# A hybrid decoder trunk on one core: output projection by seven products, gate rank inside the gate's block, norms without transposes

## The chip, the core and the metric

The program runs on one core of one Trainium2 chip. The metric is device time in microseconds (us) of one execution. The core has a matrix engine (PE), a vector engine (DVE), a scalar engine (ACT), a general engine (POOL) and a synchronisation engine (SP); each works through its own list of instructions in order, and one that waits on a semaphore holds up everything behind it on that engine. Copies between DRAM and the on-chip memory are issued by SP or POOL and carried by 16 DMA engines that all queues share.

## The reference

One layer on 1024 tokens of width 2048, all in float32. Three groups of heads read the same normed input through one wide projection `w_in`; their outputs are normed per head, gated, and go through one output projection. Then come a cross attention over 256 memory tokens and a last norm.

```python
h = rmsnorm(x, norm_mix)
(sb_q, sb_k, sb_v, sb_g, gla_q, gla_k, gla_v, gla_r, gla_g,
 sgu_u, sgu_v, sgu_g) = split(h @ w_in)          # widths 4 x 1024, 256, 256, 512, 16, 512, 3 x 512
o_sb  = stick_breaking_attention(sb_q, sb_k, sb_v)               # 8 heads of 128
log_alpha = log_sigmoid(gla_r @ w_gla_gate_up + b_gla_gate) / 16
o_gla = gla_chunked(gla_q, gla_k, gla_v, log_alpha)
o_sgu = chunked_sgu(gelu(sgu_u), gelu(sgu_v), sgu_norm, w_sgu, b_sgu)
mix  = rmsnorm per head (concat[o_sb, o_gla, o_sgu])
gate = silu(concat[sb_g, gla_g, sgu_g])
x = x + (mix * gate) @ w_out                                     # 1024 x 2048 by 2048 x 2048
x = x + memory_cross_attention(rmsnorm(x, norm_xattn), rmsnorm(mem, norm_mem), w_xq, w_xkv, w_xo)
return rmsnorm(x, final_norm)
```

## The kernel before

**Arithmetic.** Every float32 operand of a large product is kept as a rounded part and a remainder (`split_to`: a copy on ACT, then a subtraction on DVE), and a product is three matmuls (`mm3`), each with a stationary block of 128x128 and 512 moving columns. Weights come from DRAM in pieces of 128x512 (256 KB) on SP's queue into three buffers `wr`, and are split into three pairs of buffers `wh`, `wl`.

**Stages.** `natural(acts, w3, c0, width, evac)` computes 512 columns of `acts @ w3` for all 1024 tokens in eight PSUM banks: 16 steps, one weight piece each, of 24 matmuls with the activations stationary. The program runs through (1) the loads of the transposed input, its norm, and the first values of two head groups in 64 half-steps of 12 matmuls, one weight piece each; (2) five natural blocks over `w_in`: the second half of the attention's values, then `su`, `sv`, `sg` and the gate `gg`, each stored to DRAM from SBUF; (3) keys and values of the memory; (4) column blocks for the other groups, woven with their chunked work, where `gla_rank` computes the 16 rank columns with 64 matmuls whose output has 32 rows; (5) eight attention heads; (6) the output projection in four chunks of 512 columns, whose result plus `x` is stored to `x2_scr` (`evac_chunk`); (7) the second norm, which loads `x2` rows back, scales them on DVE and turns them with 128 PE transposes (`norm2_turn`), half of it inside the last chunk and half inside the first query block; (8) two query blocks, the cross attention, and 32 output steps of 12 matmuls with a norm of each group of 128 rows (`out_step`, `out_norm_step`).

**What sets the order.** `weave` writes PE's order by hand: a list of steps, and tasks that are due at a step number (`later`). PE keeps exactly that order. The order on the other engines, SP's queue of DMA issues among them, is made by a scheduler when the program is built: an instruction stands where that scheduler expects it to be ready, which is not always where the code has it. At run time each engine keeps the order that it was given.

Of the kernel before, what the change touches and what calls it, by code (L numbers as in the profile page):

```python
# [8 lines left out]
F32 = mybir.dt.float32  # L9
# [8 lines left out]
P = 128  # L18
# [23 lines left out]
def trunk(ctx, tc, x, mem, w_in, w_gla_gate_up, sgu_norm, w_sgu, w_out, w_xq, w_xkv, w_xo, final_norm,  # L42
          xT, memT, cols_in, out, dbg=None):
# [3 lines left out]
    x2d, mem2d, out2d = x[0], mem[0], out[0]  # L47
# [9 lines left out]
    actp = ctx.enter_context(tc.tile_pool(name="actp", bufs=16))  # L57
# [12 lines left out]
    def slot(dt=F32R, name="slot"):  # L70
        return actp.tile([P, 4, 512], dt, tag="act", name=name)
# [31 lines left out]
    layout = (("out", 16), ("xat", 16), ("mem", 16), ("bg", 2), ("bs", 4))  # L103
# [156 lines left out]
    def natural(acts, w3, c0, width, evac, order=range(KT)):  # L260
        for load, steps in row_block(acts, w3, c0, width, evac, [(k, range(ST)) for k in order]):
            load()
            steps[0]()

    class Stage:


        def __init__(self, name, bufs=1):
            self.args, self.pool = dict(name=name, bufs=bufs), None
# [11 lines left out]

    v_scr = [scratch(f"v_scr{s}", [P, 8, 2, P]) for s in range(ST)]
    nat_scr = {nm: [scratch(f"{nm}{s}", [P, 512]) for s in range(ST)] for nm in ("su", "sv", "sg", "gv", "gg")}
    kt_scr = [scratch(f"kt{m}", [P, 4, P]) for m in range(2)]
# [4 lines left out]
    x2_scr = [scratch(f"x2{s}", [P, D]) for s in range(ST)]  # L289
# [47 lines left out]
    with tc.tile_pool(name="st0", bufs=2) as st0:  # L337
# [87 lines left out]
        natural(hT, w_in3, SB_V + 512, 512, evac_v(st0, 512, 4, tag="vt"))  # L425
        last = [None]
        for nm, c0, func in (("su", SG_U, AF.Gelu_apprx_tanh), ("sv", SG_V, AF.Gelu_apprx_tanh),
                             ("sg", SG_G, AF.Silu), ("gg", GL_G, AF.Silu)):
            natural(hT, w_in3, c0, 512, evac_nat(nm, func))
# [120 lines left out]
    def gla_open():  # L550
# [15 lines left out]
        wup = gp.tile([32, 256], F32, name="wup")  # L566
        for i in range(2):
            sp.dma_start(wup[16 * i:16 * i + 16, :], w_gla_gate_up[0])
        wr = gp.tile([P, KT, 16], F32, tag="e", name="wr16", bufs=3)
        sp.dma_start(wr, w_in3[:, :, GL_R:GL_R + 16])  # L570

        wr2 = gp.tile([P, KT, 32], F32R, tag="e", name="wr32", bufs=3)
        split_to(wr2[:, :, 0:16], wr2[:, :, 16:32], wr)
# [5 lines left out]
        rr = gp.tile([32, S], F32, name="rr")  # L579
        gl.update(masks=masks, ind=ind, wup=wup, wr2=wr2, state=state, ql=ql, rr=rr)  # L580

    def gla_rank(h, k0):
        if k0 == 0:
            gl["rb"] = bank("z")
        b = gl["rb"]
        for k in range(k0, k0 + 4):
            for i in range(2):
                mm(b[:32, :], gl["wr2"][:, k, :], hT.at(k, h)[i], k == 0 and i == 0, k == KT - 1 and i == 1)
        if k0 + 4 == KT:
            dve.tensor_copy(gl["rr"][:, h * 512:h * 512 + 512], b[:32, :])  # L590
# [150 lines left out]
    for j in range(8):  # L741
        later(43 + j, gla_rank, j // 4, 4 * (j % 4))
# [182 lines left out]
    ss_x2 = const.tile([P, ST, 4], F32, name="ss_x2")  # L925
    op = Stage("op", 3)
    mT = Operand()
    order = list(range(8, 16)) + list(range(8))

    def mixed(k, h):  # L930

        sl = slice(h * 512, h * 512 + 512)
        if (k // 4, h) not in mT.t:
            mT.t[k // 4, h] = (slot(), slot())
        if k >= 8:
            t = wraw.tile([P, 512], F32, tag="wr", name="mraw")
            sp.dma_start(t, mix_scr[k - 8][:, sl])
        else:
            t = op.tile([P, 512], F32, tag="mraw", name="mraw", bufs=4)
# [36 lines left out]
    for n in (1, 2):  # L976
        natural(mT, w_out3, n * 512, 512, evac_chunk(n), order=order)
# [218 lines left out]
```

## Time and profile before

| | |
|---|---|
| three timed runs | 2161.27, 2162.8, 2168.68 us; median 2162.8 |
| profiled execution | 2166.49 us, its span in the trace 2164.6 us |
| granted PE clock, mean | 0.995 |
| PE busy | 2108.2 us, 97% of the span, 10000 records |
| weight loads on PE | 1735.2 us, beside the matmuls |
| DVE, ACT, POOL busy | 1077.2, 890.6, 186.3 us |
| moved by DMA | 242.66 MB, mean 112 GB/s |

Busy times of different engines overlap and do not add up to the span. A matmul's record is longer than the distance to the next one, since matmuls are pipelined; the distance between starts is what a matmul costs. Loading a weight block runs beside the matmul before it.

### The profile page before, as it was taken

To read this page: it belongs to the slowest core of one execution; us is meant where nothing else is said; L and a number is where in the kernel's file an instruction comes from. 1 tells how busy PE (TensorE), PEld (TensorE's weight loads), DVE (VectorE), ACT (ScalarE), POOL (GpSimd) and SP (SyncE) were. 2 spreads that over 40 slices of the span, in tenths; PEclk is the share of its full clock that TensorE was granted. 3 is DMA by queue.
4 is the path that set the end of the run, shared out by engine and by line. 5 is a ranking of instruction groups with operands and counts; after the bars stand their busy time and mean duration, and the time that the engine had idled before them with its cause. 6 is when DMAs were issued, how large, how long until landed. Compare 5 with 4: busy or idle time off the path is not lost.

```text
span 2164.6 us, 27461 instructions
## 1 busy us (share of the span) xinstructions
PE 2108.2 (97%) x10000; PEld 1735.2 (80%) x10000; DVE 1077.2 (50%) x1978; ACT 890.6 (41%) x1975; POOL 186.3 (9%) x271
## 2 busy tenths in 40 slices
PE   7999999999999999999999999999999999999997
PEld 6788888888887767878888888888877878888886
DVE  8593121111115737375377677776753121377675
ACT  7463111121225432342366665665654121356553
POOL 6200000000000210101110111111012000000001
PEclk9999999999999999999999999999999999999999
DMA  6486132221237521312221222222267231665632
GB/s 210 137 266 210 49 127 59 78 88 49 88 101 235 171 52 40 107 34 89 78 62 52 56 64 57 59 57 56 80 203 234 63 123 49 199 198 168 223 118 98
DMA packets 183111, 242.66 MB, mean 112 GB/s; under 512 B 17568, under 2 KB 99008, under 8 KB 180800
## 3 DMA queue, kind: packets, MB, share of 16 engines
q1 hardware_dynamic: 173760, 232.52, 34.5%
q0 software_dynamic: 9216, 8.39, 1.7%
q8 instruction: 79, 1.29, 0.3%
q14 instruction: 56, 0.46, 0.1%
HBM read 191.56 MB, written 49.28 MB: 111 GB/s over the span
## 4 chain that ended last, share of the span: by engine, by line
PE 43%; DVE 9%; ACT 5%; issue 5%; DMA 2%; POOL 1%; SPq 0%; DVEq 0%; POOLq 0%; ACTq 0%
PE pj L166 31%; PE z L166 6%; PE av L166 4%; DVE a L839 1%; PE tr L171 1%; DVE a L845 1%; ACT t L833 1%; ACT t L834 1%; PE tr L166 1%; DVE t L835 1%; ACT a L846 1%; DMA mraw<-mix 1%; DVE ql L637 1%; ACT t L832 1%; DVE wl L135 1%
## 5 line engine op out<-in xcount | busy, mean ns | idle before, releaser
L135 DVE TENSOR_TENSOR wl<-wr,wh 128x512 fp32r<-128x512 f32 x408 | 297.4, 730 | 715.8 <-ACT wh L134 707.8
L166 PE MATMUL pj<-slot,wh 128*128 128x512 f32 x2048 | 577.1, 398 | 0.5 <-DVE qT L135 0.5
L134 ACT CAST wh<-wr 128x512 fp32r<-128x512 f32 x408 | 252.2, 618 | 747.6 <-PE av L166 518.8
L166 PE MATMUL pj<-wh,slot 128*128 128x512 f32 x1536 | 478.6, 393 | 0.0
L166 PEld LDWEIGHTS pj<-slot,wh 128*128 128x128 f32 x2048 | 370.2, 189 | 71.1 <-issue 2.3
L166 PEld LDWEIGHTS pj<-wh,slot 128*128 128x128 f32 x1536 | 291.8, 190 | 60.6 <-DVE slot L139 0.3
L166 PE MATMUL pj<-slot,wl 128*128 128x512 f32 x1024 | 327.2, 390 | 0.0
L166 PE MATMUL pj<-wl,slot 128*128 128x512 f32 x768 | 304.2, 396 | 17.3 <-DVE wl L135 10.7
L166 PEld LDWEIGHTS pj<-slot,wl 128*128 128x128 f32 x1024 | 192.2, 188 | 42.5
L166 PE MATMUL z<-wh,slot 128*128 128x512 f32 x640 | 197.9, 390 | 0.1
L166 PEld LDWEIGHTS pj<-wl,slot 128*128 128x128 f32 x768 | 145.8, 190 | 51.6 <-DVE wl L135 15.1
L166 PEld LDWEIGHTS z<-wh,slot 128*128 128x128 f32 x640 | 120.2, 188 | 25.8 <-DVE slot L135 0.9
L166 PE MATMUL z<-wl,slot 128*128 128x512 f32 x320 | 125.6, 392 | 4.8 <-DVE xo L956 3.5
L835 DVE SCALAR_TENSOR_TENSOR t<-z,t 128x384 f32<-128x384 f32 (+2 forms) x96 | 53.5, 557 | 94.0 <-ACT t L834 93.9
L166 PE MATMUL tr<-wh,slot 128*128 128x512 f32 x320 | 98.6, 389 | 0.0
L166 PE MATMUL av<-wh,slot 128*128 128x512 f32 x320 | 98.5, 389 | 0.0
L846 ACT ACTIVATE a<-a 128x384 f32<-128x384 f32 (+2 forms) x96 | 50.4, 525 | 114.9 <-DVE a L845 114.8
L166 PE MATMUL pj<-slot,oT 128*128 128x512 f32 x384 | 90.9, 392 | 0.0
L166 PEld LDWEIGHTS pj<-slot,oT 128*128 128x128 f32 x384 | 70.9, 188 | 14.2
L166 PEld LDWEIGHTS z<-wl,slot 128*128 128x128 f32 x320 | 60.1, 188 | 19.7 <-DVE xo L956 4.3
L166 PE MATMUL z<-kT,qT 128*128 128x512 f32 (+3 forms) x288 | 71.2, 355 | 0.0
L166 PEld LDWEIGHTS tr<-wh,slot 128*128 128x128 f32 x320 | 60.1, 188 | 12.4
(252 smaller groups left out, 2647.7 us busy)
## 6 DMA issues: line engine op xcount, KB each, us to landing
wr<-in_w_in_dram SPq DMA_DIRECT2D x256, 256.0 KB, 2.8
wr<-in_w_out_dram SPq DMA_DIRECT2D x88, 256.0 KB, 3.1
xt<-in_xT_dram SPq DMA_DIRECT2D x64, 256.0 KB, 3.9
v_scr<-vt SPq DMA_DIRECT2D x16, 512.0 KB, 3.6
wr<-in_w_xkv_dram SPq DMA_DIRECT2D x32, 256.0 KB, 3.1
v<-v_scr POOLq DMA_DIRECT2D x64, 128.0 KB, 2.8
xr<-in_x_dram SPq DMA_DIRECT2D x32, 256.0 KB, 5.8
x<-xo SPq DMA_DIRECT2D x32, 256.0 KB, 4.0
```

The lines of the kernel that those rows point to most:

```text
L134: act.copy(hi, src)
L135: eng.tensor_tensor(out=lo, in0=src, in1=f32(hi), op=ALU.subtract)
L166: i = pe.matmul(o, l, r, start=start, stop=stop)
L171: i = pe.transpose(o, i_, ident)
L637: dve.tensor_tensor(out=gl["ql"][r_, :, hh, :].rearrange("p c (b i) -> p c b i", i=h), in0=gl["q"][r_, :].rearrange("p (c b i) -> p c b i" ...
L832: act.activation(tw, z, AF.Abs)
L833: act.activation(tw, tw, AF.Exp, scale=-1.0)
L834: act.activation(tw, tw, AF.Ln, bias=1.0)
L835: dve.scalar_tensor_tensor(out=tw, in0=z, scalar=0.0, in1=tw, op0=ALU.max, op1=ALU.add)
L839: dve.tensor_tensor_scan(out=aw[:, ::-1], data0=tw[:, ::-1], data1=tw[:, ::-1], initial=init, op0=ALU.add, op1=ALU.max)
L845: dve.tensor_tensor(out=aw, in0=z, in1=aw, op=ALU.subtract)
L846: act.activation(aw, aw, AF.Exp)
```

## The change

**Output projection.** The product of the 1024x2048 activations with the 2048x2048 weights is cut into 2x2 quarters and done by seven products of quarters instead of eight (`PRODUCTS`), in the order 4, 7, 1, 5, 3, 6, 2. Weights are now the stationary operand and the output comes out transposed. Each product has 16 steps of 12 matmuls of 512 columns. Five of the seven need a sum or difference of two weight quarters. Those are made ahead, in 80 pieces: two loads of 256 KB on SP into `ws` (three buffers for each of the two), an add on POOL (L464), and a store of 256 KB to `sums_scr` issued by POOL (L465). The code asks for one piece at each step of the natural blocks (`beside`). Five products need a sum of two activation quarters, which POOL makes (`as`). Four accumulators per token half and column half lie in SBUF, are preloaded with the transposed input (`sum_open`) and take each product's result by DVE (`collect`, 96 adds); banks of a product's second half first go through a copy on ACT (`ev`).

**Gate rank.** The 16 rank columns lie beside the gate's 512 in `w_in`, so the gate block becomes two blocks of 272 and 256 columns; 8 transposes bring the rank columns into the form that the 64 matmuls gave.

**Norms.** `x2` arrives transposed, so the second norm's gain is applied while it is split (`arrive2`), the sum of squares is made by POOL adds and one matmul with a matrix of ones per half (`scales2`), and the scale itself is applied after the query product. The output steps are transposed too: 64 pairs of products with 256 moving columns, and a last norm by matmuls with ones. The program writes its output transposed.

The instruction lists of the two programs differ by these counts on PE: 958 fewer matmuls of 512 columns with 128 rows of output, 64 fewer with 32 rows, 128 fewer transposes of 128x128, 8 more transposes with 16 rows of output, 384 more matmuls of 272 columns and 1168 more of 256 columns. DMAs issued by SP go from 892 to 1098.

```diff
+    sums_scr = {p: scratch(f"sums{p}", [8, P, 1024]) for p in PRODUCTS if PRODUCTS[p][3]}
...
-        natural(hT, w_in3, SB_V + 512, 512, evac_v(st0, 512, 4, tag="vt"))
+        pending = []
+        sums = Stage("sums", 3)
+        sums.open()
+
+        def sum_pieces():
+            for kk in range(8):
+                for prod in (4, 7, 1, 3, 6):
+                    for j in range(2):
+                        ts = []
+                        for i, (kh, nh) in zip("ab", PRODUCTS[prod][2]):
+                            t = sums.tile([P, 512], F32, tag=f"sum{i}", name="ws")
+                            c0 = nh * 1024 + j * 512
+                            sp.dma_start(t, w_out3[:, kh * 8 + kk, c0:c0 + 512])
+                            ts.append(t)
+                        pending.append((ts, prod, kk, j))
+                        yield
+
+        def sum_store():
+            ts, prod, kk, j = pending.pop(0)
+            pool.tensor_tensor(out=ts[0], in0=ts[0], in1=ts[1], op=PRODUCTS[prod][3])
+            pool.dma_start(sums_scr[prod][kk, :, j * 512:j * 512 + 512], ts[0])
+
+        pieces = sum_pieces()
+
+        def beside():
+            next(pieces, None)
+            if len(pending) > 1 or pending and not pieces.gi_frame:
+                sum_store()
+        natural(hT, w_in3, SB_V + 512, 512, evac_v(st0, 512, 4, tag="vt"), beside=beside)
         for nm, c0, func in (("su", SG_U, AF.Gelu_apprx_tanh), ("sv", SG_V, AF.Gelu_apprx_tanh),
-                             ("sg", SG_G, AF.Silu), ("gg", GL_G, AF.Silu)):
-            natural(hT, w_in3, c0, 512, evac_nat(nm, func))
+                             ("sg", SG_G, AF.Silu)):
+            natural(hT, w_in3, c0, 512, evac_nat(nm, func), beside=beside)
+        def evac_gg(lead):
+            def f(s, b):
+                t = st0.tile([P, 512], F32, tag="nt", name="nt", bufs=4)
+                if lead:
+                    dve.tensor_copy(t[:, 256:272], b[:, :16])
+                    sp.dma_start(rank_scr[:, s, :], t[:, 256:272])
+                last[0] = act.activation(t[:, :256], b[:, lead:], AF.Silu)
+                c = 0 if lead else 256
+                sp.dma_start(nat_scr["gg"][s][:, c:c + 256], t[:, :256])
+            return f
+        natural(hT, w_in3, GL_R, 272, evac_gg(16), beside=beside)
+        natural(hT, w_in3, GL_G + 256, 256, evac_gg(0), beside=beside)
+        while pending:
+            sum_store()
+        sums.close()
...
-    def gla_rank(h, k0):
-        if k0 == 0:
-            gl["rb"] = bank("z")
-        b = gl["rb"]
-        for k in range(k0, k0 + 4):
-            for i in range(2):
-                mm(b[:32, :], gl["wr2"][:, k, :], hT.at(k, h)[i], k == 0 and i == 0, k == KT - 1 and i == 1)
+    def gla_rank(h):
+        tp = bank("z")
+        for i in range(4):
+            flip(tp[:16, i * P:i * P + P], gl["rank"][:, 4 * h + i, :])
+        dve.tensor_copy(gl["rr"][:, h * 512:h * 512 + 512], tp[:16, :])
...
     def mixed(k, h):
 
         sl = slice(h * 512, h * 512 + 512)
-        if (k // 4, h) not in mT.t:
-            mT.t[k // 4, h] = (slot(), slot())
+        t = mix_at(k, h)
         if k >= 8:
             sp.dma_start(t, mix_scr[k - 8][:, sl])
-            t = op.tile([P, 512], F32, tag="mraw", name="mraw", bufs=4)
-            g_ = op.tile([P, 512], F32, tag="graw", name="graw", bufs=4)
+            g_ = op.tile([P, 512], F32, tag="ev", name="graw")
             sp.dma_start(t, on_scr[k][:, sl])
             sp.dma_start(g_, g_scr[k][:, sl])
             last[0] = act.activation(g_, g_, AF.Silu)
             pool.tensor_tensor(out=t, in0=t, in1=g_, op=ALU.mult)
-        split_to(*mT.at(k, h), t)
-
-    def evac_chunk(n):
-        xr = {}
-
...
+    def sum_open(sh, nh):
+        for g in range(2):
+            sp.dma_start(home(SUM[sh, nh][g], "sum", F32), xT3[:, 8 * nh + 4 * g:8 * nh + 4 * g + 4, sh * 512:sh * 512 + 512])
+    FINAL = {(0, 0): 5, (0, 1): 3, (1, 0): 2, (1, 1): 2}
...
+    def prepare_weight(u, prod, kk, j, early):
...
+        def fetch():
+            t = op.tile([P, 512], F32, tag="ra", name="ra") if j and not early else \
+                wraw.tile([P, 512], F32, tag="wr", name="ra")
+            c0 = j * 512
+            if sign:
+                sp.dma_start(t, sums_scr[prod][kk, :, c0:c0 + 512])
+            else:
+                (kh, nh), = quarters
+                sp.dma_start(t, w_out3[:, kh * 8 + kk, nh * 1024 + c0:nh * 1024 + c0 + 512])
+            raws.append(t)
...
+        def split():
+            if j and not early:
+                hl = tuple(op.tile([P, 512], F32R, tag=f"w1{i}", name="w1", bufs=2) for i in "hl")
...
+            wp[u] = hl
+        later(u - (3.2 if early else 6), fetch)
+        later(u - (1.2 if early else 2.8), split)
+
+    def prepare_operand(u, prod, kk):
...
+        def add():
+            st.append(op.tile([P, 512], F32, tag="as", name="as", bufs=2))
+            a, b = (mix_at(kh * 8 + kk, sh) for sh, kh in quarters)
+            pool.tensor_tensor(out=st[0], in0=a, in1=b, op=sign)
...
+        def split():
+            src = st[0] if sign else mix_at(quarters[0][1] * 8 + kk, quarters[0][0])
+            hl = tuple(op.tile([P, 512], F32R, tag=f"a{i}", name="a") for i in "hl")
+            split_to(hl[0], hl[1], src)
+            ap[u] = hl
+        if sign:
+            later(u - 5, add)
+        later(u - 3, split)
...
+    def product_pass(u0, prod, js, tags):
...
+        def step(u, kk, j):
+            w = wp.pop(u)
+            a = a4(kk) if prod == 4 else ap[u - j]
+            for i in range(4):
+                b = 4 * j + i
+                if kk == 0:
+                    banks[b] = bank(tags[b % len(tags)])
+                mm3(banks[b], cut(w, i * P, i * P + P), a, kk == 0, kk == 7)
+                if kk == 7:
+                    collect(prod, b, banks[b], len(js) == 2 and j == 1)
...
+    def collect(prod, b, z, through):
+        if through:
+            t = op.tile([P, 512], F32, tag="ev", name="ev")
+            act.copy(t, z)
+            z = t
+        for (sh, nh), sign in PRODUCTS[prod][4]:
+            d = sum_at(sh, nh, b)
+            dve.tensor_tensor(out=d, in0=d, in1=z, op=sign)
+            if FINAL[sh, nh] == prod:
+                n = 8 * nh + b
+                sp.dma_start(x2_scr[sh][n // 4][:, n % 4], d)
+
+    FOUR, EIGHT = ("pj",) * 4, NAT
+    groups += product_pass(END, 4, (0,), FOUR) + product_pass(END + 8, 4, (1,), ("z", "z", "tr", "av"))
+    for n, prod in enumerate((7, 1, 5, 3, 6)):
+        groups += product_pass(END + 16 + 16 * n, prod, (0, 1), EIGHT)
+    groups += product_pass(W2, 2, (0, 1), EIGHT)
+    for j in range(8):
+        later(END - 12 + j, mixed, 8 + j, 1)
+        later(END - 3 + 0.6 * j if j < 4 else END + j - 3.5, lambda j=j: split_to(*a4(j), mix_at(8 + j, 1)))
+        later(END + 2 + j, mixed, 8 + j, 0)
+        later(END + 18 + j, mixed, j, 0)
+        later(END + 34 + j, mixed, j, 1)
+    later(END + 3, sum_open, 0, 0)
+    later(END + 5, sum_open, 1, 0)
+    later(END + 18, sum_open, 0, 1)
+    later(END + 20, sum_open, 1, 1)
...
+    def arrive2(k, h):
+
+        st = op if h == 0 else xp
+        t = st.tile([P, 512], F32, tag="x2t", name="x2t", bufs=3 + h)
+        sp.dma_start(t, x2_scr[h][k // 4][:, k % 4])
+
+        def f():
+            hi, lo = h2_at(k, h)
+            split_gain(hi, lo, t, col("xat", k))
+            if k == 0:
+                sq_sum[h] = xr.tile([P, 512], F32, tag="acc", name="acc")
+                act.activation(sq_sum[h], t, AF.Square)
+            else:
+                sq = st.tile([P, 512], F32, tag="sq", name="sq", bufs=3)
+                act.activation(sq, t, AF.Square)
+                pool.tensor_tensor(out=sq_sum[h], in0=sq_sum[h], in1=sq, op=ALU.add)
...
+    def scales2(h):
+        st = bank("z")
+        mm(st, ones_f, sq_sum[h], True, True)
+        t = xr.tile([P, 512], F32, tag="t", name="t")
+        R[h] = xr.tile([P, 512], F32, tag=f"R{h}", name="R")
+        inverse_rms(R[h], st, sq_sum[h], R[h], t)
...
-                mm3(banks[h], cut(w[k], h * P, h * P + P), h2T.at(k, half), k == 0, k == KT - 1)
+                mm3(banks[h], cut(w[k], h * P, h * P + P), h2_at(k, half), k == 0, k == KT - 1)
             if k == KT - 1:
                 for h in range(4):
+                    u = xa.tile([P, 512], F32, tag="e", name="qu", bufs=3)
                     t = tuple(xa.tile([P, 512], F32R, tag="qT", name="qT", bufs=8) for _ in range(2))
-                    split_to(t[0], t[1], banks[h])
+                    dve.tensor_tensor(out=u, in0=banks[h], in1=R[half], op=ALU.mult)
+                    split_to(t[0], t[1], u)
...
+    def out_step(p, jj):
         b = bank("pj")
...
+        for i in range(2):
+            j = 2 * jj + i
+            for h in range(4):
+                c = (h % 2) * 256
+                mm3(b[:, i * 256:i * 256 + 256], cut(wxo[h, j // 4], j % 4 * P, j % 4 * P + P),
+                    cut(oT[p, h // 2], c, c + 256), h == 0, h == 3)
+        x3 = fin_at(p, jj // 2)[:, jj % 2 * 2:jj % 2 * 2 + 2]
+        b3 = b.rearrange("p (a s) -> p a s", a=2)
+        dve.tensor_tensor(out=x3, in0=b3, in1=x3, op=ALU.add)
...
+        acc, sq = temp(p % 2), temp(2 + (jj % 2 if jj < 7 else 2 + p % 2))
+        to = acc if jj == 0 else sq
+        act.activation(to.rearrange("p (a s) -> p a s", a=2), x3, AF.Square)
+        if 0 < jj < 7:
+            pool.tensor_tensor(out=acc, in0=acc, in1=sq, op=ALU.add)
+        for i in range(2):
+            act.activation(x3[:, i], x3[:, i], AF.Copy, scale=col("fin", 2 * jj + i))
+
+    def out_norm_step(p):
+        st = bank("z")[:, :256]
+        parts = [t[:, i * 256:i * 256 + 256] for t in (temp(p % 2), temp(4 + p % 2)) for i in range(2)]
+        for n, t in enumerate(parts):
+            mm(st, ones_f, t, n == 0, n == 3)
+        a, c = temp(6), temp(7)
+        v, y, t, r = a[:, :256], a[:, 256:], c[:, :256], c[:, 256:]
+        inverse_rms(r, st, v, y, t)
+        for g in (2, 0, 1, 3):
+            x3 = fin_at(p, g)
+            (pool if g == 2 else dve).tensor_tensor(out=x3, in0=x3, in1=r.unsqueeze(1).to_broadcast([P, 4, 256]), op=ALU.mult)
...
```

How SP's queue stands, first before: the rows from the end of the half-steps into the natural blocks. `wr` is a weight piece, `vt` a stored value tile; a number behind an x counts equal rows in sequence.

```order
L447 DMA mr<-in_mem_dram 128x512 x2
L145 DMA wr<-in_w_in_dram 128x512 x8
L303 DMA v_scr_91<-vt 128x1024
L303 DMA v_scr_92<-vt 128x1024
L145 DMA wr<-in_w_in_dram 128x512
L303 DMA v_scr_93<-vt 128x1024
L303 DMA v_scr_94<-vt 128x1024
L145 DMA wr<-in_w_in_dram 128x512 x15
```

The same queue now, from the first of those value stores of this pair on; `ws` is one of the two loads of a piece of the weights' sums.

```order
L321 DMA v_scr_96<-vt 128x1024
L321 DMA v_scr_97<-vt 128x1024
L148 DMA wr<-in_w_in_dram 128x512
L457 DMA ws<-in_w_out_dram 128x512
L321 DMA v_scr_98<-vt 128x1024
L321 DMA v_scr_99<-vt 128x1024
L457 DMA ws<-in_w_out_dram 128x512
L148 DMA wr<-in_w_in_dram 128x512
L457 DMA ws<-in_w_out_dram 128x512 x4
L148 DMA wr<-in_w_in_dram 128x512
L457 DMA ws<-in_w_out_dram 128x512 x6
L148 DMA wr<-in_w_in_dram 128x512
```

Between two weight pieces there now stand 4 to 6 loads for the sums, not the two that the code asks for at a step. Counted along the whole queue, the first `ws` stands just ahead of the 55th `w_in` load, 21 of the 160 ahead of the 65th (the first of the natural blocks), 80 ahead of the 80th, and all 160 ahead of the 98th.

On DVE, at the joint of two chunks before: weight splits (L135), and the adds that empty the banks (L956).

```order
L135 TENSOR_TENSOR wl<-wr,wh 128x512 x15
L956 TENSOR_TENSOR xo<-pj,xr 128x512 x4
L956 TENSOR_TENSOR xo<-z,xr 128x512
L135 TENSOR_TENSOR wl<-wr,wh 128x512
L956 TENSOR_TENSOR xo<-z,xr 128x512
```

At the joint of the products 1 and 5 now: splits of weights (`w_`) and of an operand (`a`) on L138, and the adds into the accumulators (`slot`) on L1104.

```order
L138 TENSOR_TENSOR w_15378<-ra,w_15377 128x512
L138 TENSOR_TENSOR w_15338<-ra,w_15337 128x512
L1104 TENSOR_TENSOR slot<-slot,pj 128x512 x8
L138 TENSOR_TENSOR a<-as,a 128x512
L1104 TENSOR_TENSOR slot<-slot,ev 128x512 x8
L138 TENSOR_TENSOR w_15400<-ra,w_15399 128x512
```

Sixteen adds now stand nearly together, with one split among them, where eight stood with one split among them.

272 lines of the change are left out of this document (133 added, 139 removed).

## The prediction

> **What bounds the kernel now.** I read the page of the profile first: the busy shares, then the span in 40 slices.
>
> ```profile
> span 2164.6 us, 27461 instructions
> PE 2108.2 (97%) x10000; PEld 1735.2 (80%) x10000; DVE 1077.2 (50%) x1978; ACT 890.6 (41%) x1975; POOL 186.3 (9%) x271
> ...
> PE   7999999999999999999999999999999999999997
> ...
> PEclk9999999999999999999999999999999999999999
> DMA  6486132221237521312221222222267231665632
> ```
>
> PE is busy in all but the first and last slice at full granted clock, so a matmul taken away is worth its distance to the next one, as long as what feeds PE keeps up. Next I cut the span into stages: natural blocks, column blocks and attention, output projection, query blocks, the rest.
>
> ```profile
> 205.00:640.00 435.00, 434.73 (x1916) 359.03 (x1915) 61.78 (x90) 74.12 (x122) 0.00 (x0) 1.00 0.25 80
> 640.00:1565.00 925.00, 907.58 (x4570) 746.36 (x4569) 582.25 (x1103) 459.52 (x1051) 104.73 (x208) 1.00 0.29 81
> 1565.00:1939.00 374.00, 364.44 (x1639) 298.41 (x1638) 133.51 (x260) 126.58 (x285) 21.92 (x19) 1.00 0.48 149
> 1939.00:2049.00 110.00, 109.07 (x566) 91.80 (x565) 80.64 (x190) 68.24 (x180) 0.00 (x0) 1.00 0.60 199
> 2049.00:2165.00 116.00, 103.96 (x524) 87.80 (x522) 70.59 (x144) 46.83 (x135) 10.73 (x8) 0.97 0.32 120
> ```
>
> Columns are the stretch, its length, busy PE, weight loads, DVE, ACT, POOL, then clock, DMA share and GB/s. The natural blocks, where the change makes the weights' sums, have an idle POOL and a quarter of the DMA engines in use. PE never waits there: 434.73 of 435. The output projection waits little, too:
>
> ```profile
> PE z L166 <- DVE xo L956: 3.5, 2, 1.9
> PE pj L166 <- DVE wl L135: 1.1, 1, 1.1
> PE z L171 <- DVE slot L139: 1.0, 2, 0.6
> ```
>
> **The change in PE work.** Prices come from the timeline: ACT's weight splits follow PE's steps in a natural block, and PE's own rows give the narrow forms.
>
> ```profile
> 341.21 0.62 ACT L134 CAST wh<-wr 128x512 fp32r<-128x512 f32 x1 [4.82 <-PE av L166]
> 346.65 0.62 ACT L134 CAST wh<-wr 128x512 fp32r<-128x512 f32 x1 [4.82 <-PE av L166]
> 1996.80 0.88 PE L166 MATMUL z<-slot,qT 128*128 128x256 f32 x6
> 1997.52 0.40 PE L166 MATMUL pj<-slot,wh 128*128 128x512 f32 x1
> 1904.00 0.60 PE L171 MATMUL tr<-ident,x2t 128*128 128x128 f32 x4
> 1904.43 0.60 PE L171 MATMUL av<-ident,x2t 128*128 128x128 f32 x4
> L166 PE MATMUL z<-slot,wr 128*32 128x512 f32 x64 | 15.9, 391 | 0.1
> 97.44 1.96 PE L166 MATMUL pj<-squares,ones_f 128*128 128x512 f32 x4
> 878.67 0.60 PE L166 MATMUL z<-v,kdn 128*128 128x256 f32 x2
> 878.92 0.58 PE L166 MATMUL pj<-slot,wh 128*128 128x512 f32 x1
> ```
>
> - A step of 24 matmuls of 512 columns takes 346.65 − 341.21 = 5.44 us, 0.227 each. Six of 256 columns take 0.72, 0.12 each. Four transposes take 0.43, 0.108 each.
> - Output projection: 4 chunks × 16 × 24 = 1536 matmuls before, 7 × 16 × 12 = 1344 now: 192 × 0.227 = −43.5 us.
> - Second norm: 128 × 0.108 = −13.8.
> - Rank: 64 matmuls whose records are as long (391 ns) as those of full ones, −14.5, and 8 transposes, +0.9: −13.6.
> - Gate block: 384 of 512 columns become 384 of 272 and 384 of 256. The trace has no 272; on the line between 0.12 and 0.227 it is 0.127. 384 × (0.127 + 0.12 − 0.227) = +7.7; with 272 at 0.12, the nearest row, +5.1, with 0.14, +12.7.
> - Output steps: 768 × 0.12 − 384 × 0.227 = +5.0.
> - Sums by ones in float32: a 512-wide one leaves two records, 0.98 each by the 1.96 row, and its starts are closer: I take 0.86. A 256-wide one lies between 0.25 (to the next start) and 0.60 (end of both records): 0.43. 2 × 0.86 + 16 × 0.43 = +8.6, ends 5.7 and 11.6.
>
> Together −49.6, from −55 to −41. The narrow matmuls are where a rule can be held to the trace. The Trainium skill, page "TensorE: Matmul & The Clock Gate", section "Back-to-back issue gap", gives N/2.4 + 2.5 ns for an isolated matmul, 109 ns for 256; this trace has 120, and the 1152 matmuls of 256 columns in the gate's second block and the output steps would cost 12.7 us less by the rule, an estimate; the measured row stands.
>
> **Other engines of the output projection.** Per product DVE has 16 weight splits, 8 operand splits and 16 adds in 16 × 2.72 = 43.5 us.
>
> ```profile
> L135 DVE TENSOR_TENSOR wl<-wr,wh 128x512 fp32r<-128x512 f32 x88 | 62.6, 713 | 186.3 <-ACT wh L134 181.4 <-DMA xr<-in_x_dram 4.7
> L956 DVE TENSOR_TENSOR xo<-pj,xr 128x512 f32<-128x512 f32 x19 | 11.8, 682 | 0.0
> L134 ACT CAST wh<-wr 128x512 fp32r<-128x512 f32 x88 | 54.5, 619 | 181.0 <-PE av L166 143.9 <-PE pj L166 24.2 <-DMA wr<-in_w_out_dram 9.8
> L944 POOL TENSOR_TENSOR mraw<-mraw,graw 128x512 f32<-128x512 f32 x16 | 21.0, 1315 | 54.1 <-DMA wr<-in_w_out_dram 26.6 <-ACT graw L943 22.9 <-DVE wl L135 4.5
> L812 POOL DMA_DIRECT2D v<-v_scr x64 | 35.0, 549 | 146.6 <-PE av L166 143.8 <-issue 2.3
> ```
>
> DVE: 24 × 0.71 + 16 × 0.68 = 27.9, 64%. ACT: 24 × 0.62 and 8 bank copies at most as long, 19.8. POOL: 8 × 1.32 = 10.5. None is the bound on average. At a joint, 16 adds and a split keep DVE for 11.6 us, while the splits behind them were due 2.8 steps (7.6 us) ahead. The adds begin two matmul groups before the step ends (about 2 us) and two more weight splits stand ahead of them, so the next weights come about when PE wants them: 0 to 3 us per joint, five joints. The 5.6 us of waits quoted above go with the old code. I set the two against each other at 0; ends −5.6 and +9.4. The 40 POOL adds, the reloads of x2 (32 pieces of 256 KB instead of 8 MB in rows) and the first weights of product 4 lie beside PE work of 2.72 us a step; if that cover went, each add would show 1.32.
>
> **Tail.** The end follows the chain after the last matmul:
>
> ```profile
> 2152.98 0.02 issue
> 2153.00 0.70 DVE slot L1112
> ...
> 2155.97 0.75 DVE slot L1127
> ```
>
> It runs 11.6 us to 2164.6. Now the scale is made on 256 columns instead of one (six instructions some 0.2 longer), three DVE products are 1024 wide instead of 512 (0.75 more each, the row doubled) and the last store is larger. That is 1.2 + 2.2, less about 0.9 for a product that POOL now does alone beside them: +2.5, ends 0 and +5.
>
> **The sums' loads.** The queue lists decide this. SP's 160 `ws` loads all stand between the 55th and the 98th weight load, and a `ws` load waits until its buffer, three pieces back, is stored. Weight loads stand behind it on SP.
>
> ```profile
> 164.11 0.45 SPq L145 DMA_DIRECT2D wr<-in_w_in_dram  x1
> L166 PE MATMUL pj<-wl,mh x64: 392/396/505, 640.2 to 690.4; 128*128 128x512 f32 x64
> 112.00:136.00 24.00, 24.00 (x106) 19.48 (x105) 23.15 (x38) 16.22 (x28) 0.00 (x0) 1.00 0.94 311
> 136.00:154.00 18.00, 18.00 (x82) 14.89 (x80) 18.00 (x30) 10.11 (x17) 0.00 (x0) 1.00 0.85 262
> 1940.00:1950.00 10.00, 10.00 (x47) 8.23 (x46) 5.37 (x25) 3.57 (x15) 0.00 (x0) 1.00 1.02 353
> wr<-in_w_in_dram SPq DMA_DIRECT2D x10, 256.0 KB, 4.0
> gv<-gv SPq DMA_DIRECT2D x4, 256.0 KB, 4.3
> wr<-in_w_in_dram SPq DMA_DIRECT2D x6, 256.0 KB, 3.5
> su<-nt SPq DMA_DIRECT2D x8, 256.0 KB, 2.3
> ```
>
> Weight load 55 is issued at 164.1. The memory's products start at 640.2, so the natural blocks start at 640.2 − 80 × 5.44 = 205.0, and load 97, the 33rd of theirs, is used at 205.0 + 32 × 5.44 = 379.1 and must land some 4 us sooner. That leaves 211 us. In it must pass 80 × 0.786 = 62.9 MB for sums, 43 × 0.262 = 11.3 for weights, 12 × 0.524 = 6.3 of stored values: 80.5 MB. At 311 GB/s, the densest stretch of small loads, that takes 259 us, 48 too long; at 353 (1 MB loads among them), 228, 17 too long; at 262, 307, 96 too long. The three buffers set a second pace: load 3.5 to 4.0, second issue 0.43, add 1.32, issue 0.55, store 2.3 to 4.3 (the store rows above), together 8.1 to 10.6 us for three pieces, 2.7 to 3.5 each: 216 to 283 us, 5 to 72 too long. The nearest row is 311 GB/s, since it mixes pieces of this size with stores; the buffers' middle, 250, says 39. I take 44, ends 5 and 96.
>
> **Sum.** −49.6 + 0 + 2.5 + 44 = −3, against the profiled execution's 2166.5: 2163.4. That execution stood 3.7 above the median of 2162.8, so for the median of runs I say 2160.
>
> **Rivals.**
> - The DMA carries it all (hidden sums). For it: the natural blocks use 0.25 of the DMA engines, 80 GB/s, and POOL is idle in them. Then 5 us remain: 2160 − 39 = 2121. The Trainium skill, page "DMA: Bandwidth & Descriptors", section "Bandwidth", gives 425 GB/s for a long transfer by one core alone; 80.5 MB would take 189 us, within the 211, an estimate. Against it: no stretch here of 10 us shows more than 353, and the buffers' pace does not care for the rate. Chance 0.15.
> - Slower: the store is what a `ws` load waits for, and weights stand behind that wait. With stores of POOL's queue at 4.3 us and loads at 4.0 under full DMA, and the 262 GB/s row, the stall is 72 to 96: 2188 to 2212. It decides from a stall of 53 us on (47 saved and 6.5 to measure), 3.3 us a piece. Chance 0.15.
> - DVE at the joints: if the weights behind 16 adds come 5 us late five times, the forecast becomes 2185. For it: the lists have the adds ahead of the splits. Against it: 64% busy. Chance 0.10.
> - The forecast's own case, a stall of 17 to 72: 2133 to 2188. Chance 0.60.
>
> **Chances.** About 0.3%, 6.5 us, is what a measurement of this kernel can tell from no change. The forecast's case gives faster when the stall stays below 40 (0.27), slower above 54 (0.14), between them the same (0.19). With hidden sums (faster 0.15), slow stores (slower 0.15) and joints (slower 0.08, same 0.02): faster 0.42, same 0.21, slower 0.37. The range reaches into hidden sums and into slow stores: 2118 to 2195.
>
> **What would show it.** In the changed profile the stretch from 205 us on should show a DMA share near 0.9 and above 280 GB/s for some 200 us, PE waiting for DVE `wl` whose weights came late, and SP waiting at L457. The memory's products would begin about 640 + 8 + 44 = 692; at 650 the sums are hidden, above 730 the slow stores hold. From then to the end everything should be some 55 us shorter: the output projection near 324 instead of 374 (43.5 and half the transposes), with waits for `w0` or `w1` of at most 3 us at joints. I am wrong if PE loses more than 10 us inside the products, if a `ws` piece takes under 2.6 or over 3.5 us, or if SP's order on the chip holds weights back elsewhere.

## The result, and the profile after

The changed kernel takes 2245.26 us, median of four runs (2241.49 to 2249.34), beside 2165.74 for the kernel before: ratio 1.0367, 95% interval 1.0353 to 1.038. It is slower by 80 us where the prediction said 2160 and gave slower 0.37; the time lies above the range.

The page of the changed kernel, as before:

```profile
span 2239.8 us, 29155 instructions
...
PE 2077.1 (93%) x10428; PEld 1732.0 (77%) x10428; DVE 1182.9 (53%) x1949; ACT 936.7 (42%) x1950; POOL 482.5 (22%) x521
...
PE   7997965949999999999999999999999999998997
...
PEclk9999987979999999999999999999999999999998
DMA  6588888761222465122231222222268335454424
```

PE has less to do, 2077.1 us instead of 2108.2, but between the fourth and the ninth slice, roughly 170 to 500 us, it stands idle for much of the time, and the granted clock falls there (0.89 on average from 174 to 470). In the slices that follow it is as full as before. The natural blocks lost more than the rest won. The stretch in which the sums are made, and when the memory's products begin (640.2 before):

```profile
174.00:470.00 296.00, 217.12 (x890) 172.40 (x888) 39.95 (x53) 31.25 (x52) 146.99 (x159) 0.89 0.81 267
L464 POOL TENSOR_TENSOR ws<-ws x80: 1249/1279/1802, 173.9 to 469.3; 128x512 f32<-128x512 f32 x80
L169 PE MATMUL pj<-wl,mh x64: 392/395/505, 761.0 to 813.3; 128*128 128x512 f32 x64
```

PE is busy for 217 of 296 us. The 80 pieces take from 173.9 to 469.3 us, 3.74 each, and the memory's products begin 120.8 us late. The DMA engines are not full: share 0.81, 267 GB/s. What PE waits for in all, the largest rows:

```profile
PE pj L169 <- DVE vt L319: 39.7, 2, 25.8
PE pj L169 <- DVE wl L138: 33.5, 24, 4.8
PE pj L169 <- ACT nt L359: 26.0, 1, 26.0
PE tr L169 <- DVE vt L319: 11.2, 1, 11.2
```

Columns are the total, how often, and the longest. The larger waits are evictions of finished banks, that is copies that make a bank free again (`vt`, `nt`), 77 us in four waits; weights (`wl`) have 33.5, of which e1 below, without the sums, has 18 too. One of these waits, followed back: the timeline of SP, then what ACT and SP wait for.

```profile
340.94 10.14 SPq L457 DMA_DIRECT2D ws<-in_w_out_dram  x6
351.18 0.37 SPq L148 DMA_DIRECT2D wr<-in_w_in_dram  x1
351.65 6.46 SPq L457 DMA_DIRECT2D ws<-in_w_out_dram  x5
358.21 0.48 SPq L148 DMA_DIRECT2D wr<-in_w_in_dram  x1
358.78 0.85 SPq L321 DMA_DIRECT2D v_scr<-vt  x2
```
```profile
ACT vt L318 <- DMA v_scr<-vt: 28.2, 1, 28.2
```
```profile
SPq L457 <- DMA sums<-ws: 114.6, 56, 6.7
SPq L457 <- POOL ws L464: 60.5, 40, 3.7
```

PE has no free bank from 341 to 367 us, because ACT cannot copy one out, because its buffer `vt` is not stored. The store itself lands in 6 to 7 us. Before that it stands on SP behind eleven `ws` loads, and is issued only at 358.78; SP spends 175 us of the stretch (last rows, 174 to 470 us) waiting for the three buffers of each load of a piece, 114.6 us for a store and 60.5 for an add.

### The profile page after: what moved, and what is told of

Its sections match the earlier page's. It is cut to its first block, busy times and chain, and to the rows that moved or that the text cites. A ratio compares the mean times of both kernels' runs of the same rounds, so it can differ in the third digit from the quotient of the medians.

```text
span 2239.8 us, 29155 instructions
## 1 busy us (share of the span) xinstructions
PE 2077.1 (93%) x10428; PEld 1732.0 (77%) x10428; DVE 1182.9 (53%) x1949; ACT 936.7 (42%) x1950; POOL 482.5 (22%) x521
## 4 chain that ended last, share of the span: by engine, by line
PE 41%; DVE 9%; ACT 5%; issue 4%; DMA 2%; DVEq 0%; POOL 0%; SPq 0%; POOLq 0%; ACTq 0%
PE pj L169 28%; PE z L169 6%; PE av L169 4%; DVE a L896 1%; PE tr L169 1%; PE tr L174 1%; DVE a L902 1%; ACT t L890 1%; ACT t L891 1%; DVE t L892 1%; ACT a L903 1%; DMA x2t<-x 1%; DMA ra<-sums 1%; ACT t L889 1%; DVE ql L694 1%
## 5 line engine op out<-in xcount | busy, mean ns | idle before, releaser
L138 DVE TENSOR_TENSOR wl<-wr,wh 128x512 fp32r<-128x512 f32 (+2 forms) x336 | 245.1, 731 | 579.1 <-ACT wh L137 578.2
L137 ACT CAST wh<-wr 128x512 fp32r<-128x512 f32 (+2 forms) x336 | 200.6, 597 | 630.5 <-PE av L169 295.0
L169 PE MATMUL pj<-wh,slot 128*128 128x512 f32 (+2 forms) x1024 | 295.5, 374 | 0.0
L169 PE MATMUL pj<-wl,slot 128*128 128x512 f32 (+2 forms) x512 | 195.0, 381 | 97.8 <-DVE vt L319 39.7
L169 PEld LDWEIGHTS pj<-wh,slot 128*128 128x128 f32 x1024 | 191.3, 195 | 32.4 <-DVE slot L142 0.3
L464 POOL TENSOR_TENSOR ws<-ws 128x512 f32<-128x512 f32 x80 | 103.4, 1292 | 231.9 <-DMA wr<-in_w_in_dram 106.3
L138 DVE TENSOR_TENSOR w<-ra,w 128x512 fp32r<-128x512 f32 x112 | 96.5, 875 | 93.5 <-ACT w L137 91.4
L169 PE MATMUL z<-wh,slot 128*128 128x512 f32 (+2 forms) x512 | 143.5, 364 | 0.0
L169 PE MATMUL pj<-a,w 128*128 128x512 f32 x576 | 142.1, 395 | 0.0
L169 PEld LDWEIGHTS pj<-a,w 128*128 128x128 f32 x576 | 108.6, 188 | 25.3
```

The source lines that it names most:

```text
L137: act.copy(hi, src)
L138: eng.tensor_tensor(out=lo, in0=src, in1=f32(hi), op=ALU.subtract)
L169: i = pe.matmul(o, l, r, start=start, stop=stop)
L464: pool.tensor_tensor(out=ts[0], in0=ts[0], in1=ts[1], op=PRODUCTS[prod][3])
```

## The experiments

Ratios are against the kernel before on the same chip. "Start" is when the memory's products begin in the profile. The rows come from several chips, on which the kernel before took 2163.2 to 2166.4 us, so differences of a few us between rows are better read from the ratios.

| run | median us | ratio, 95% interval | start |
|---|---|---|---|
| changed kernel | 2245.26 | 1.0367 (1.0353 to 1.038) | 761.0 |
| e1 sums left out | 2129.01 | 0.9826 (0.9811 to 0.984) | 645.9 |
| e2 paced, other side | 2143.63 | 0.9893 (0.9878 to 0.9908) | 663.5 |
| e3 loads on POOL's queue | 2222.87 | 1.0259 (1.0242 to 1.0276) | 743.7 |
| e4 six buffers | 2169.29 | 1.0029 (1.0018 to 1.004) | 691.1 |
| e5 POOL's queue, other side | 2156.86 | 0.9961 (0.9947 to 0.9975) | 676.8 |
| e6 paced, later | 2152.19 | 0.9932 (0.9918 to 0.9946) | 663.7 |
| e7 rank alone on before | 2162.22 | 0.9983 (0.9974 to 0.9992) | 646.6 |
| e8 e6 with later scores | 2148.22 | 0.9916 (0.9901 to 0.9931) | 667.0 |
| e9 spread | 2139.19 | 0.989 (0.9874 to 0.9907) | 658.4 |
| e10 stores on ACT | 2252.55 | 1.0412 (1.0394 to 1.043) | 774.5 |
| e11 no add | 2224.34 | 1.0282 (1.0267 to 1.0298) | 743.9 |
| e12 between stores | 2131.25 | 0.9846 (0.9829 to 0.9862) | 648.4 |

**e1: is it the sums?** Products that need a sum load one quarter instead.

```diff
-        pieces = sum_pieces()
+        pieces = iter(())
...
-            if sign:
-                sp.dma_start(t, sums_scr[prod][kk, :, c0:c0 + 512])
-            else:
-                (kh, nh), = quarters
+            if True:
+                kh, nh = quarters[0]
```

> Leaves out the weights' sums: the 160 loads, 80 adds and 80 stores beside the natural blocks are gone, and the five products that need them load one quarter of the weights instead, so the output is not the reference's. In the changed kernel the memory's products begin at 761.0 us against 640.2 before; less 7.7 for the gate's blocks that is a loss of 113 us before them. Queue theory (the loss is the sums' loads standing ahead of weight loads and stores on SP): 113 us go, 2132 us, memory's products at about 648. Rival, that the loss belongs to other parts (gate blocks, narrow matmuls, DVE): over 2200. The rest of the change is then worth 2132 - 2166 = -34 by the queue theory, against -47 forecast.

Measured 2129.0, 116 us under the changed kernel, and PE is busy for all but 0.3 us from 205 us to the memory's products:

```profile
205.00:646.00 441.00, 440.68 (x2294) 379.94 (x2293) 65.27 (x113) 77.75 (x143) 0.00 (x0) 1.00 0.25 78
```

The whole loss is the sums' making, and the rest of the change is worth 36 us.

**e2: one piece to one weight load.** The same work; its order on SP is changed, and the buffers lie on the other side of the memory.

```diff
-            next(pieces, None)
+            with tc.issue_after(last_load[0].ins):
+                next(pieces, None)
...
-        sums = Stage("sums", 3)
+        sums = Stage("sums", 3, "right")
```

> All sums are made, but each piece's two loads are ordered on SP behind the weight load of their own step, so one piece goes with one weight load instead of 2.65; the buffers lie on the other side of the memory so that the memory tokens' loads need not wait for them. Queue theory: a piece has 5.44 us and needs 3.3, SP never waits for a store, within 8 us of the run without sums: 2132 to 2140. Rival, that the sums cost by their own work (POOL's adds beside DVE, 63 MB on the DMA engines): 2160 or more.

Measured 2143.6: 102 of the 116 us come back with every piece made. The expectation was missed by some 4 us; what was left is taken up in e6, e9 and e12. The share of the buffers' side was not measured alone; in the changed kernel SP's memory-token loads (L505) waited 5.9 us for the sums' buffers.

**e4, e11, e10: what sets the pace, and is it one loss or two?**

```diff
# e4
-        sums = Stage("sums", 3)
+        sums = Stage("sums", 6)
# e11
-            pool.tensor_tensor(out=ts[0], in0=ts[0], in1=ts[1], op=PRODUCTS[prod][3])
+            if prod == 4 and kk == 0:
+                pool.tensor_tensor(out=ts[0], in0=ts[0], in1=ts[1], op=PRODUCTS[prod][3])
# e10
-            sp.dma_start(v_scr[s][:, h0:h0 + nh], vt)
+            act.dma_start(v_scr[s][:, h0:h0 + nh], vt)
-                sp.dma_start(nat_scr[nm][s], t)
+                act.dma_start(nat_scr[nm][s], t)
```

> The changed kernel with six instead of three buffers for each load of a piece; SP's order stays dense, even denser (90 of the 160 loads ahead of the 81st weight load instead of 80). Queue theory with the buffers' wait as the pace: a load now waits for a store six pieces back, the pace falls from 3.3 us a piece to the bandwidth's 2.5 to 2.8, and 40 to 60 of the 113 us go: 2185 to 2205. Bandwidth rival: no change, 2235 to 2250.

> Leaves out all but two of POOL's 80 adds: each store writes the first quarter unsummed, so the output is not the reference's; loads, stores, buffers and SP's order are the changed kernel's nearly (90 of the loads ahead of the 81st weight load instead of 85). Buffer theory: a piece's buffer is held by load, add and store, three pieces in flight, so without 1.3 us of add the pace falls by 0.43 us a piece, 35 us over 80: 2205 to 2215. Bandwidth rival (the engines are full): no change, 2238 to 2250.

> The changed kernel, its stores of values and of the natural blocks' results (vt, nt) issued by ACT instead of SP; the sums' loads stay dense on SP, a little denser (98 ahead of the 81st weight load instead of 85). PE waited 78 us for evictions in the changed kernel, which wait for such stores standing behind sums' loads, and about 39 us for weights. If the two losses are separate, 50 to 78 us go: 2167 to 2195. If the pace of the pieces on SP is the one cause, and PE only waits for whatever is stuck behind it, the wait turns into one for weights: 2230 to 2250.

First and last piece in each, by POOL's adds, or by its stores where there are two adds (176.2 to 449.8; in the changed kernel the stores run from 175.9 to 470.8):

```profile
L464 POOL TENSOR_TENSOR ws<-ws x80: 1251/1294/1757, 174.2 to 393.7; 128x512 f32<-128x512 f32 x80
```
```profile
L466 POOL DMA_DIRECT2D sums<-ws x80: 539/539/733, 176.2 to 449.8; - x80
```
```profile
L464 POOL TENSOR_TENSOR ws<-ws x80: 1250/1278/1780, 171.1 to 461.0; 128x512 f32<-128x512 f32 x80
```

Six buffers (first row) shorten the 80 pieces from 295 to 219.5 us, by 76, and the kernel by 76.0 (more than the 40 to 60 expected). Without the adds (second) the pieces take 273.6 instead of 294.9, 21 less, and the kernel 20.9 less; 35 were expected, but a load then lands later (5.0 us instead of 4.3). With the stores on ACT (third) the pieces take 289.9, hardly less, and the kernel is not faster but 7 us slower. Over all rows, evictions of banks cost 55 us instead of 78, weights (`wl`) 65 instead of 39; the largest rows:

```profile
PE pj L169 <- DVE wl L138: 55.6, 25, 14.6
PE pj L169 <- DVE vt L319: 34.7, 3, 21.5
PE tr L169 <- DVE vt L319: 10.1, 2, 8.2
PE z L169 <- DVE wl L138: 9.3, 4, 4.0
```

So the two rows are not two losses to be added. PE can get no further than the weights that SP lets through, and what PE names as its wait is whatever stands behind the pieces. e10 does not prove that by itself, since its order is denser: all 160 loads are issued ahead of the 92nd weight load, where the changed kernel issues the last of them just ahead of the 98th. That puts the weights of six more steps, 33 us of PE's work, behind the pieces, which is why PE starts the memory's products later (774.5 instead of 761.0) although the pieces end sooner (461.0 instead of 469.3): 33 more, 8 less for the earlier end and 11 less for a shorter wait right after it come to 14 beside the measured 13.5. Two things then make the loss: when SP is through with the pieces, and how many steps it let through until then.

The pace of the pieces is set by the buffers, not by the engines: with six buffers, more of them are in flight, and the same engines move

```profile
174.00:394.00 220.00, 189.04 (x812) 154.66 (x811) 43.34 (x51) 30.38 (x51) 147.58 (x159) 0.93 0.98 356
```

356 GB/s at share 0.98: there the engines are nearly full. The Trainium skill, page "DMA: Bandwidth & Descriptors", section "Specifications", names about 358 GB/s as what memory gives one core. The mean of this row lies there, but it is no ceiling in this trace: 50 us of the same stretch (279 to 329) show 383. The 425 of its section "Bandwidth" is not reached by this row or by those 50 us.

**e3 and e5: another queue.** POOL issues the sums' loads; e5 also puts the buffers on the other side of the memory.

```diff
-                            sp.dma_start(t, w_out3[:, kh * 8 + kk, c0:c0 + 512])
+                            pool.dma_start(t, w_out3[:, kh * 8 + kk, c0:c0 + 512])
```

> The sums' 160 loads are issued by POOL instead of SP; their number, their buffers and their rate as the buffers allow stay. Queue theory: SP's weights and stores stand behind nothing, what is left is sharing of the 16 DMA engines: 2135 to 2160. Bandwidth rival (the DMA engines cannot carry it in that time): the loss stays, 2200 to 2245.

> The sums' loads on POOL's queue again, with their buffers on the other side of the memory. With them on POOL but on the same side, weights waited only some 10 us until 418 us, and then one gap of 82 us came, 2222.9 in all: SP's next loads of memory tokens take the place of the sums' buffers and stand, with the weights behind them, until the last piece is stored. Queue theory: without that wait 70 to 85 us go, 2138 to 2153. Bandwidth rival: the gap moves elsewhere, 2200 or more.

e3 looked like the bandwidth rival, 2222.9, but its waits said otherwise: PE lost 82 us in a single gap.

```profile
PE pj L169 <- DVE wl L138: 81.9, 1, 81.9
```
```profile
SPq L505 <- DMA sums<-ws: 92.9, 3, 89.0
```

These are PE's and SP's waits of e3 from about 400 us on: one load of memory tokens (L505), placed early by the scheduler, took over memory of the sums' buffers and held SP, and every weight behind it, until the last piece was stored. In e5 that gap is gone: 2156.9, 66 us less, 4 above what was expected. It stands 28 us above e1; what is left, with the pieces still dense, has no run of its own.

**e6, e9, e12: where the pieces may lie.** All on top of e2: e6 leaves the first block free, e9 uses only full-width steps, e12 also leaves the first steps of each block free.

```diff
# e6
-        natural(hT, w_in3, SB_V + 512, 512, evac_v(st0, 512, 4, tag="vt"), beside=beside)
+        natural(hT, w_in3, SB_V + 512, 512, evac_v(st0, 512, 4, tag="vt"))
# e9, pieces at step n of the first 64
+            want = 0 if n < 5 else 2 if n >= 16 and 3 <= n % 16 and n % 2 else 1
# e12, pieces at step k of block blk
+            if blk < 4:
+                want = 0 if k < 5 else 2 if k % 2 else 1
+            else:
+                want = 0 if k < 4 or k % 2 else 1
```

> The paced kernel (2143.6) with pieces beside the second to sixth natural block only, 80 steps for 80 pieces; the first block, whose evictions wait for 512 KB stores (PE waited 9.7 us for them), stays free. Queue theory: most of the 14.6 us that the paced kernel stands above the one without sums lies in that block and in its stores, so 2131 to 2137. Rival (each piece costs by contention, wherever it is): 2141 to 2146.

> Paced, buffers on the other side, and the pieces laid only beside steps of 5.44 us: none beside the first five steps of the first block (its evictions wait for 512 KB stores) nor beside the two gate blocks, whose steps are 2.9 to 3.0 us, shorter than a piece; 11 beside the rest of the first block, and 69 beside the next three, where six or seven steps of a block take two. Reason from the last runs: the paced late kernel laid 32 pieces beside the short steps and PE waited 7.7 us at 607 us for evictions there; the paced kernel waited 6.3 us at 207 us in the first block. Queue theory with a pace of 3.4 us a piece: both waits go, memory's products at 646 to 652, 2130 to 2136. Rival (some 15 us of contention stay, wherever the pieces are): 2141 to 2146.

> Paced, buffers on the other side, and no piece beside the first five steps of a full block or the first four of a gate block, where its predecessor's results are stored; one or two beside each later step of 5.44 us, one beside every second later step of the gate blocks. The spread kernel still waited 7.3 us at 384 us for an eviction of su, whose store stood behind sums' loads on SP. If stores behind those loads are all that is left: the wait goes, memory's products at 648 to 652, 2129 to 2134. If pieces cost by sharing the engines: 2139 or more, as the spread kernel.

e6 was a miss: 2152.2, above e2. It has 32 pieces beside the gate blocks, where e2 has 16, and their steps are shorter than a piece; PE waited 7.5 us at 607 us for an eviction. e9, 2139.2, missed by a few us and is level with e2 within the intervals; it still waited 6.9 us at 384 us for an eviction of `su`, whose stores stood on SP among the pieces' loads. e12 keeps pieces away from the steps in which a block's results are stored:

```profile
205.00:650.00 445.00, 444.37 (x2305) 382.20 (x2304) 77.75 (x114) 79.60 (x148) 149.19 (x160) 1.00 0.68 220
```

PE is busy for 444.4 of 445 us with all 80 pieces made beside it, at 220 GB/s and with POOL adding and issuing for 149 us. 2131.25 us, ratio 0.9846: 1.5% under the kernel before, with every piece made. The kernel without sums stands 2 us lower by the medians and 4 by the ratios, and the two intervals overlap. So of the 116 us nearly all was the sums' place in the queue and the side of their buffers, and what the sums cost by their own work is not clear of the noise.

**e7: the gate rank alone**, on the kernel before.

```diff
+        natural(hT, w_in3, GL_R, 272, evac_gg(16))
+        natural(hT, w_in3, GL_G + 256, 256, evac_gg(0))
...
-        later(43 + j, gla_rank, j // 4, 4 * (j % 4))
+        later(46 + h, gla_rank, h)
```

> The kernel before with the gate rank alone moved inside the gate's block. By the matmuls' distances (measured since: 0.125 us for 272 columns, 0.120 for 256): 384 x (0.125 + 0.120 - 0.227) = +6.9 and -13.6 for 64 matmuls less 8 transposes: -6.7 us, ratio 0.997. Rival: the 64 matmuls filled waits of other work in the woven blocks, so that only the +6.9 is seen: ratio 1.003.

Ratio 0.9983, interval 0.9974 to 0.9992: 3.7 us less, between the two expectations and nearer to the full price. The start moves by 6.4, near the 6.9; after it 10 us are won in the profiles instead of 13.6.

**e8: the first scores later**, on e6.

```diff
-            t = W2 + (33, 40.2, 49.5, 56.7)[pair] + 3.6 * hp
+            t = W2 + (34.6, 41, 49.5, 56.7)[pair] + 3.6 * hp
```

> The paced and late kernel with the first scores of the cross attention 1.6 steps later (and the second pair 0.8): PE stood 3.6 us there until the scaled queries were split, and ran at half clock for a while after. If that wait is a matter of its place: 5 to 6 us under the paced late kernel, 2126 to 2131. If the chain just ends later: same as it, within 2 us.

2148.2 beside 2152.2, intervals that overlap; from the start on, the two profiles differ by 1 us (1481.4 and 1482.4). The 3.6 us wait went, and transposes that did not wait before now wait 4.6 us for DVE's `pT`, in four waits: the chain ends no sooner.

## Why the prediction was wrong

**The sums' loads: right in kind, wrong in size.** The prediction had the queue, the buffers and the stall, took 44 us and 96 as the far end; the loss is 116 by runs, 115 by the start (761.0 − 645.9 of e1). The step that failed is the pace. The 44 stand for 80 pieces in 255 us, between 250 by the buffers (8.1 to 10.6 us for three pieces) and 259 by bandwidth, against a window of 211; measured are 295, 3.74 each. That is 40 us. It counted from 164, when weight load 55 is issued, and had no term for filling the first piece: the first load is issued at 162.6, as it said, but the piece's second load stands behind value stores until 167.8, and the first add is at 173.9, 10 us after 164. The pieces then end at 469 where the weights behind them were due at 375: 44 + 40 + 10 = 94 us. What came after the last piece was not in the sum either: the bank copies of `su` still waited until 489.6, behind memory-token work on ACT whose loads stood behind the pieces too (26.0 us, `ACT nt`). PE goes on at 490.2 with the step that was due at 379.1, 111 us late, and some 4 us more of waits before 761.0 make the 115.

The far end of 96 comes near the 94 by luck: it stood for full engines at 262 GB/s, and the engines were not full (share 0.81). Its own far end by the buffers was 72. The signs that the prediction gave came true: 3.74 us a piece is over the 3.5 at which it called itself wrong, and a start at 761 is above the 730 from which slow stores were to hold.

Why 3.74 and not 3.2: loads landed in 4.3 us and stores of sums in 4.2 (medians of the page), where 3.5 to 4.0 and 2.3 to 4.3 were assumed and a middle taken (44, between 39 and 48). With 0.43, 1.3 and 0.55 for issue, add and issue that alone makes 10.8 us for three pieces, 3.6 each. The rest lies where value stores of 512 KB come in between: there ten pieces took 41 to 49 us, elsewhere 34 to 36.

**What was queued behind the wait.** The prediction named weights alone. Stores and memory-token loads stand on SP too. A late store is a full bank: 51 of the 77 us of evictions (`vt`). The other 26 (`nt`) are the copies behind the memory tokens. While pieces were still coming, such waits mostly took the place of waits for weights (in e10 the one fell by 23 us and the other rose by 26), though SP itself lost 11.8 us to `vt` (L321); the 26 us came after the last piece, and there the omission cost in full.

**The rivals.** Slow stores, chance 0.15, 2188 to 2212, was the right mechanism (114.6 us of SP's waits are for `sums` stores), still too small. Hidden sums, 0.15, is false for this order and true within the noise for e12's. One argument against it was a misreading: the trace before does have 10 us above 353 GB/s, 395 from 2044 to 2054, with loads of 1 MB. Full engines as the limit are out: share 0.81 here, 0.98 with six buffers.

**The rest of the change.** Forecast −47, measured −36 by runs (e1), −39.5 in the profiles. By stage, e1 against before: start +5.7 (forecast +7.7); from there to the query blocks 1233.9 instead of 1298.8, −64.9 (−64.0); first query step to first output step 115.0 instead of 109.7, +5.2 (−5.2); output steps 115.3 instead of 103.9, +11.4 (+11.9); tail +3.1 (+2.5). The seven products, the rank and half of the transposes came out together as said; the rank alone gave 10 us instead of 13.6 (e7), so the rest gave a little more. The query blocks are the miss, 10.4 us. The rows are e1's, the waits those from 1900 to 1945; `kr` are the memory's keys as loaded, `qu` the scaled queries:

```profile
1880.00:1995.00 115.00, 107.48 (x506) 87.28 (x505) 91.16 (x135) 67.14 (x135) 23.15 (x15) 0.97 0.66 207
```
```profile
PE pj L169 <- DVE wl L138: 3.7, 4, 2.1
PE z L169 <- issue: 3.6, 1, 3.6
1937.23 1.62 PE L169 MATMUL z<-slot,qT 128*128 128x256 f32 x6 [3.64 <-issue]
```
```profile
1932.04 2.04 SPq L1199 DMA_DIRECT2D kr<-kt  x4
1933.69 0.68 DVE L138 TENSOR_TENSOR qT<-qu,qT 128x512 fp32r<-128x512 f32 x1
1936.44 0.69 DVE L138 TENSOR_TENSOR slot<-kr,slot 128x512 fp32r<-128x512 f32 x1 [0.26 <-ACT slot L137]
```

The scale after the query product was costed at nothing, and no work was named that hides it. It adds four DVE products ahead of the first scores on an engine that is busy for 91 of 115 us there. PE waited 3.7 us for weights and 3.6 at the first scores, and its granted clock fell to 0.78 around that (six 256-wide matmuls in 1.42 us at 1937 instead of 0.72). The 3.6 us do not end with the scaled queries, whose last split is over at 1934.4, but with the first split of the memory's keys (`kr`), over at 1937.1, 0.1 us before PE goes on. In the changed code the keys' raw tiles share the three buffers `e` with the scaled queries (`qu`), where they had buffers of their own before; their loads are issued at 1932.0, as soon as the second of the queries is split. In the kernel before they were issued at 1981.9 and split by 1987.5, ahead of the queries. So part of the miss is a shared buffer and not the scale's own work; no run gave the keys their own buffers or left the scale out, and how the 10.4 us divide stays open. Joints of the products cost little, as set: 4.1 us of waits for `w` in e1.

## What to carry to other kernels

In-order queues make neighbours of work that has nothing to do with each other: before a batch of prefetches goes on a queue, list everything that stands behind each of its waits, stores included, and compare the chip's time for one item (load, work and store over the buffers it has) with the time until the next thing in that queue is due. Here the built order had five or six loads, some 2.7 pieces, to a step in its dense parts, where 1.5 pieces fit (5.44 us by 3.74). An order edge to a load of the same step, with the buffers where no later load needs their place, brought back 102 of the 116 us, and keeping clear of the steps that store results nearly all the rest. When one change moves a waiter to another queue and the time stays, look at when the batch ends and how much work stands behind its end, not at the waits.

## What was not expected of the hardware

- Same engines, same pieces: 267 GB/s with three buffers and 356 with six. With more transfers in flight the rate rose by a third, and landing stretched from 2.7 us (weights alone) to 5.6 in the six-buffer run.
- A 272-column matmul stands 0.125 us from the next, close to the 0.127 taken from the line; 256 columns 0.12, as before.
- In the seven products the matmuls of the `pj` and `z` banks stand 0.232 us apart (median) where those of the other banks and of the old projection had 0.227, some 4 us over the stage; why was not tried.
